# Token shift in two scaled terms: one on ScalarE into PSUM, one on VectorE

## The chip, the core and the metric

The kernel runs on one core of a Trainium2 chip. Its engines are TensorE (PE, matmul, with the weight load PEld shown apart), VectorE (DVE), ScalarE (ACT), GpSimd (POOL) and SyncE (SP, which issues the DMAs here). The metric is device time in microseconds of one execution; lower is better. Times of several runs are compared by their median.

## The reference, cut to what matters

One step of a decoder trunk with one layer, for a prompt of 1024 rows and 8 sample rows, all float32: a feed-forward block, a mixing block, a second feed-forward block. The mixing block projects each row to 3328 columns; the last 1792 of them, `pb`, feed a recurrent part, and this part begins with the token shift:

```python
def rwkv7_time_mix(pb, prev, s0, lp):
    shifted = jnp.concatenate([prev[:, None, :].astype(pb.dtype), pb[:, :-1]], axis=1)
    xs = pb + (shifted - pb) * lp['mu_shift']
    r, k, v, xw, xa, xg = jnp.split(xs, B_SPLITS, axis=-1)
    w = -jax.nn.softplus(-(lp['w0'] + jnp.tanh(xw) @ lp['w2']).astype(f32)) - 0.5
    a = jax.nn.sigmoid((lp['a0'] + xa @ lp['a2']).astype(f32))
    g = jax.nn.sigmoid(xg) @ lp['g2']
    ...
    s, y = wkv_scan(s0.astype(f32), r, decay, k, v, kk, a)
```

Each value is mixed with the value of the row before, with a weight `mu_shift` per column. The 1792 columns are 14 tiles of 128: four each of r, k and v, one that holds xw and xa, and one for xg.

## The kernel before, in words

Activations lie with features on the 128 partitions and tokens along the free axis. The prompt is cut into two halves of 512 rows (the first also carries the 8 samples). Each half goes through a first feed-forward phase (phases 0 and 1 of the trunk), the projection, the token shift and the recurrent part, the attention, the output projection, and a second feed-forward phase (trunk phases 2 and 3). Float32 products are made of three matmuls on split operands: weights come in as `raw`, ACT casts a high part, and POOL or DVE subtracts it for the low part (the tile `wts_w` for the feed-forward weights, `lin_w` for the projections).

Work is written as streams (generators): `trunk`, `wts`, `lin`, `proj`, `pre`, `tail`, `lora`, `job0` and `job1`, `attn`, `outn`, `dec` and so on. A planner (`Kern.run`, line 475) takes instructions from the streams and fixes the order on every engine before anything runs. It works with estimated costs (`price`, line 378) and, from the second pass on, with a latest time for each instruction, worked out backwards from the pass before (`latest`, line 564). `PASSES` (line 93) is the number of planning passes; the order of the last one is emitted. `BIAS` (line 94) adds microseconds to the latest times of a named stream, where the number is the how-manieth stream of that label it is (`tail1` is the second tail stream); a smaller latest time is taken first. Each engine runs its queue in the planned order. Because every instruction is emitted at one place, all have line 317 in the profile; tiles tell them apart, as `<stream>_<tile>`.

A PSUM tile is taken with `ps` or `ps2` (lines 238 and 245). Within a stream it comes from that stream's list of banks, in the order in which the program asks; a new tile in a bank waits for all uses of the tile before it. The jobs' first part has the bank `dec`, which the streams `pre`, `stats`, `decb` and others use too; later a job changes to `aux0` or `aux1`.

The token shift is `mixed` (line 1627). It is called twice in `s_lora` (line 1640) and three times in each `job` (line 1663, for k, r and v), four jobs to a half: 14 times a half, 28 in all. It loads a row tile from the scratch `PT` into E (one column more than 512, so that `E[:, 0:HS]` is the row before), POOL subtracts, and DVE scales and adds. The result goes to `out`, one of the tiles named `mix_T` in the profile, or `bset_la` and `bset_sg` for the two of `s_lora`. Within a job, the k tile comes first; the sums of squares for the key's norm go to a tile of the bank `dec`, and an inverse square root is worked out there in small DVE steps (line 1697); then the r tile is shifted (line 1698), the inverse norms are broadcast (line 1701) and turned by four transposes into another tile of that bank (line 1705); the v tile is shifted (line 1712) before the bonus term's matmul takes the bank (line 1716). The lock `front` lets one job, or `s_lora`, at a time use the shared input tiles.

Of the kernel before, what the change touches and what calls it, by code (L numbers as in the profile page):

```python
# [17 lines left out]
AF = mybir.ActivationFunctionType  # L18
ALU = mybir.AluOpType
# [3 lines left out]
P = 128  # L23
# [6 lines left out]
HS = 512  # L30
# [15 lines left out]
NB = 14  # L46
# [43 lines left out]
MW = 1  # L90
MARG = 0
SLACK = 0.02
PASSES = 2
BIAS = {"trunk2": 310, "outn3": -60, "outb0": 30, "pre2": -3, "outn0": -30, "rows0": -30, "job00": -10, "job03": 10, "stats0": 10, "dec0": 10, "wts3": 3, "pre3": -30, "mix1": -60, "lora1": 3, "attn11": 3, "tail2": 3}
SHIFT = {}
RESAT = 3
GROUPS = {(0, 10): [[0, 1, 2], [3, 4], [5, 6, 7], [8, 9]], (3, 6): [[0, 1, 2], [3], [4, 5]],
          (0, 8): [[0, 1, 2], [3, 4], [5], [6, 7]], (0, 6): [[0, 1, 2], [3], [4, 5]], (3, 4): [[0, 1], [2, 3]], (3, 8): [[0, 1, 2], [3, 4], [5], [6, 7]]}
# [29 lines left out]
def col(t):  # L128

    return t + TD * (t >= HS)  # L130
# [79 lines left out]
class Kern:  # L210
# [99 lines left out]
    def put(self, eng, op, fn, a, k):  # L310
# [14 lines left out]
        if o.late is not None:  # L325
            o.late += BIAS.get(st.part, 0) + sum(d for a, b, d in self.shift.get(st.part, ()) if a <= o.key[1] < b)
        self.price(o, op, a, k, outs[0], ins)
# [385 lines left out]
    def columns(self):  # L713

        nc, I = self.nc, self.I
        rows = self.E[:, :P]
        t = self.T(self.const, [P, P], "cols")
        r = 0
        for nm in ("n_ffn1_post", "n_mix_pre", "n_mix_post", "n_ffn2_pre", "n_ffn2_post",
                   "subln", "mu_shift", "w0", "a0", "k_k", "k_a", "r_k", "ln_x_w", "ln_x_b"):  # L720
            a = I[nm]
            if len(a.shape) == 3:
                a = a.rearrange("o h d -> o (h d)")
            k = a.shape[1] // P
            nc.sync.dma_start(rows[r:r + k, :], a[0].rearrange("(k p) -> k p", p=P))
            self.col[nm] = (t, r, k)
            r += k
        yield
        pt = self.ps2()
        nc.tensor.transpose(pt[:, :r], rows[:r], self.ident[:r, :r])  # L730
        nc.vector.tensor_copy(t[:, :r], pt[:, :r])
        for nm, k in (("n_ffn1_post", 0.5), ("n_ffn2_post", 0.5), ("subln", 1.0 - LAM_INIT), ("w0", 0.5), ("a0", 0.5)):
            nc.vector.tensor_scalar(self.vecs(nm), self.vecs(nm), k, None, ALU.mult)
        self.omka = self.T(self.const, [P, 4], "omka")
        nc.vector.tensor_scalar(self.omka, self.vecs("k_a"), -1.0, 1.0, ALU.mult, ALU.add)
        yield
# [57 lines left out]
    def stats(self, src, rb, tmp=("sqs", 1), **kw):  # L794

        for k in range(KT):
            self.square_sum(rb, src[k], k, self.tmp(*tmp, rb.shape[-1]), **kw)
        self.rstd(rb)

    def pair(self, k, src, gain, x):  # L800
# [573 lines left out]
    def s_loadx(self, half):  # L1374
# [28 lines left out]
        if half == 0:  # L1403
            yield ("wait", ("loaded", 0, "up", RESAT, None))
        for hf in range(2):
# [133 lines left out]
    def s_mix(self, half):  # L1539

        pool = self.pool
        yield ("wait", "setup")
        for m in (24, 25):
            yield ("wait", ("done", half, m))
        yield ("wait", ("staged", 1 + half))
        self.front = self.stage()
        self.spawn(self.s_lora(pool, half), "lora", 0)
        for i in range(4):
            self.spawn(self.s_job(pool, i, half), f"job{i % 2}", 0, "dec")
        self.sets = []  # L1550
        for j in range(2):
            if half:
                yield ("wait", "proj1")
            self.job_buffers(half, j)
            self.signal(("sets", half, j))
        for what in (f"jobs0_{half}", f"jobs1_{half}", f"rope{half}") + ("dec_b",) * half:
            yield ("wait", what)
        self.a_buffers(pool, half)
        self.spawn(self.s_prepare(pool, half), "prep", 0, "cb")
        for b in range(2):  # L1560
            self.spawn(self.s_attend(pool, half, b), f"attn{b}", 0, f"m{2 + b}", f"aux{b}")
        self.spawn(self.s_finish(pool, half), "fin", 0, "cb")
        if half:
            self.spawn(self.s_states(pool), "states", 2, "cb")
        self.spawn(self.s_out(half), "outb" if half else "out", 0, "m2", "m3")
# [61 lines left out]
    def mixed(self, pool, m, s, out, tag):  # L1627

        nc = self.nc
        t0 = col(s * HS)  # L1630
        E = self.first(tag, 1)
        nc.sync.dma_start(E[:, 1:], self.PT[12 + m][:, t0:t0 + HS])
        if s == 0:
            nc.gpsimd.memset(E[:, 0:1], 0.0)
        else:
            nc.sync.dma_start(E[:, 0:1], self.PT[12 + m][:, HS - 1:HS])
        nc.gpsimd.tensor_tensor(out, E[:, 0:HS], E[:, 1:], ALU.subtract)
        nc.vector.scalar_tensor_tensor(out, out, self.vec("mu_shift", m), E[:, 1:], ALU.mult, ALU.add)

# [297 lines left out]
    def s_decode_a(self):  # L1937
        yield ("wait", "setup")
        yield ("wait", ("staged", 1))
        yield ("wait", ("done", 0, 3))  # L1940
        yield ("wait", "lead")
        yield from self.a_decode()
        self.spawn(self.s_decode_b(), "decb", 1, "dec", ahead=8)

    def s_decode_b(self):
        yield ("wait", "proj0")
        take = self.arena(self.T(self.pool, [P, W_DEC], "dreg"))
        yield from self.b_decode(take, take, take(TD, C))
        self.signal("dec_b")

    def s_states(self, pool):

# [586 lines left out]
@with_exitstack  # L2539
def hymba_kernel(ctx, tc, I, O, late=None, dry=False):  # L2540
    K = Kern(ctx, tc, I, O, late, dry)
    K.setup()
    DR = lambda shape, tag: K.dram.tile(list(shape), F32, tag=tag, name=tag)
    K.res = DR([P, KT, NT], "res")
    K.PTall = DR([26, P, NT], "PT")
    K.PT = [K.PTall[m] for m in range(26)]
    K.YMall = DR([8, P, NT], "YM")
    K.YM = [K.YMall[m] for m in range(8)]
    K.Md = [DR([4, NC, 32, 32], f"Md{b}") for b in range(2)]
    K.Xd = [DR([4 * NC, 8, 4, 32], f"Xd{b}") for b in range(2)]  # L2550
    K.Dd = DR([160, P], "Dd")
    K.Qd = DR([32, P], "Qd")
    K.Ld, K.Lg = [DR([NF, P, D], f"Ld{i}") for i in range(2)], [DR([2, 12, P, D], f"Lg{i}") for i in range(2)]
    K.Li, K.Lo = DR([26, P, KT, P], "Li"), DR([KT, P, KT, P], "Lo")
    K.drams = {t.tensor.name: (tuple(t.shape), []) for t in (K.res, K.PTall, K.YMall, *K.Md, *K.Xd, K.Dd, K.Qd, O[3], *K.Ld, *K.Lg, K.Li, K.Lo)}
    K.c2 = K.const
    K.rows4 = K.T(K.const, [P, 1040], "rb")
    K.rb, K.prb = K.rows4[:, :520], K.rows4[:, 520:]
    K.E = K.T(K.const, [P, 520], "E")
    K.W, K.x, K.xt, K.ab = {}, {}, {}, {}  # L2560
    K.side = 0
    K.spawn(K.s_loadx(0), "ldx", 0, "cb", "dec")
    K.spawn(K.s_rownorm(0), "ssx", 0, RB)
    K.spawn(K.s_loadx(1), "ldxb", 3, "cb")
    K.spawn(K.s_rownorm(1), "ssxb", 3, RB)
    for ph in range(4):
        K.spawn(K.s_pre(ph), "pre", 0, "dec")
        if ph > 1:
            K.spawn(K.s_stats(ph), "stats", 1, "dec")
    K.asides = {}  # L2570
    for label in ("wts", "lin"):
        K.spawn(K.s_aside(), "keep", 0)
        K.asides[label] = K.streams[-1]
    K.spawn(K.s_weights(), "wts", 1)
    K.spawn(K.s_trunk(), "trunk", (0, 3), "m0", "m1")
    K.spawn(K.s_setup(), "setup", 2, "cb")
    for half in range(2):
        K.spawn(K.s_project(half), "proj", 0, "m2", "m3")
        K.spawn(K.s_rope(K.pool, half), "rope", 2)
        K.spawn(K.s_mix(half), "mix", 2)  # L2580
    K.spawn(K.s_decode_a(), "dec", 1, "cb", ahead=24)
    K.run()
    if dry:
        raise Planned(K.predicted, K.latest())
# [40 lines left out]
```

## Time and profile before

| | |
|---|---|
| median of 3 runs | 2302.5 us (2299.95 to 2308.67) |
| the profiled execution, its own time | 2294.3 us |
| its span, first to last instruction | 2292.3 us |
| mean granted TensorE clock | 0.991 |
| PE busy | 2228.0 us (97%) |
| DVE busy | 1556.5 us (68%) |
| ACT busy | 1078.0 us (47%) |
| POOL busy | 1021.6 us (45%) |

The profile is of one execution, so its times belong to the 2294.3 us of that execution. A line of a group gives the engine, the operation, output and inputs by tile names, shapes and count, then busy time, mean length of one, and the idle time of the engine just before them with what ended it. A line of a tile's instructions gives shortest, median and longest length in ns. A busy share of an engine is a mean over stages with different limits, so the stretches around an instruction say more than the page's first line.

### The profile page before, as it was taken

To read this page: it belongs to the slowest core of one execution; us is meant where nothing else is said; L and a number is where in the kernel's file an instruction comes from. 1 tells how busy PE (TensorE), PEld (TensorE's weight loads), DVE (VectorE), ACT (ScalarE), POOL (GpSimd) and SP (SyncE) were. 2 spreads that over 40 slices of the span, in tenths; PEclk is the share of its full clock that TensorE was granted. 3 is DMA by queue.
4 is the path that set the end of the run, shared out by engine and by line. 5 is a ranking of instruction groups with operands and counts; after the bars stand their busy time and mean duration, and the time that the engine had idled before them with its cause. 6 is when DMAs were issued, how large, how long until landed. Compare 5 with 4: busy or idle time off the path is not lost. (4 is left out here: it accounts for less than half of the span.)

```text
span 2292.3 us, 42829 instructions
## 1 busy us (share of the span) xinstructions
PE 2228.0 (97%) x15857; PEld 1985.3 (87%) x15857; DVE 1556.5 (68%) x3545; ACT 1078.0 (47%) x2231; POOL 1021.6 (45%) x846
## 2 busy tenths in 40 slices
PE   8999999999999999999899999999999999999998
PEld 7999999799887778988787867777788888999998
DVE  5477988756766687477866367665667356777776
ACT  5433443634354365434552145443665556544444
POOL 3344565534343566356543124333443254544443
PEclk9999999999999999999899999999999999999999
DMA  6423334344334576655679643324745847544543
GB/s 205 132 86 100 102 93 130 104 146 140 109 113 108 170 228 204 218 151 151 194 200 225 169 138 114 111 75 121 205 122 168 273 145 249 148 114 130 148 138 111
DMA packets 476295, 343.15 MB, mean 150 GB/s; under 512 B 82457, under 2 KB 424061, under 8 KB 476088
## 3 DMA queue, kind: packets, MB, share of 16 engines
q1 hardware_dynamic: 475480, 338.82, 50.8%
q8 instruction: 125, 2.05, 0.4%
q0 software_dynamic: 320, 1.08, 0.1%
q14 instruction: 82, 0.67, 0.1%
q10 hardware_dynamic: 288, 0.52, 0.1%
HBM read 278.98 MB, written 61.38 MB: 148 GB/s over the span
## 5 line engine op out<-in xcount | busy, mean ns | idle before, releaser
L317 PE MATMUL trunk_m<-trunk_xl,wts_w 128*128 128x256 f32 (+2 forms) x2700 | 459.4, 321 | 6.9 <-DVE trunk_xl L317 6.2
L317 POOL TENSOR_TENSOR wts_w<-wts_raw,wts_w 128x1024 fp32r<-128x1024 f32 (+2 forms) x162 | 314.4, 1948 | 318.1 <-ACT wts_w L317 279.4
L317 PE MATMUL trunk_m<-pre_X,wts_w 128*128 128x512 f32 (+3 forms) x2400 | 439.9, 335 | 5.7 <-POOL wts_w L317 2.8
L317 PEld LDWEIGHTS trunk_m<-trunk_xl,wts_w 128*128 128x128 f32 x2700 | 382.3, 189 | 42.3 <-DVE trunk_xl L317 7.9
L317 PEld LDWEIGHTS trunk_m<-pre_X,wts_w 128*128 128x128 f32 x2400 | 352.6, 190 | 48.2 <-issue 6.8
L317 PE MATMUL trunk_m<-pre_T,wts_w 128*128 128x512 f32 (+3 forms) x1848 | 362.8, 347 | 5.2 <-DVE trunk_xl L317 2.4
L317 ACT CAST wts_w<-wts_raw 128x1024 fp32r<-128x1024 f32 (+2 forms) x293 | 244.2, 848 | 237.9 <-PE trunk_m L317 162.1
L317 PEld LDWEIGHTS trunk_m<-pre_T,wts_w 128*128 128x128 f32 x1848 | 286.9, 190 | 43.7 <-issue 3.8
L317 DVE TENSOR_TENSOR trunk_xl<-trunk_xl,trunk_m 128x256 f32<-128x256 f32 (+2 forms) x351 | 165.8, 489 | 77.3 <-PE trunk_m L317 76.1
L317 PE MATMUL proj_m<-tail_xl,lin_w 128*128 128x256 f32 (+1 forms) x1248 | 168.5, 290 | 2.3 <-POOL lin_w L317 1.9
L317 PEld LDWEIGHTS proj_m<-tail_xl,lin_w 128*128 128x128 f32 x1248 | 155.6, 190 | 11.3 <-issue 7.0
L317 POOL TENSOR_TENSOR trunk_xl<-trunk_t,trunk_xl 128x512 fp32r<-128x512 f32 (+3 forms) x86 | 94.5, 1100 | 149.9 <-ACT trunk_xl L317 149.7
L317 PE MATMUL proj_m<-tail_T,lin_w 128*128 128x512 f32 (+1 forms) x672 | 153.1, 386 | 4.9 <-ACT tail_T L317 3.8
L317 PEld LDWEIGHTS proj_m<-tail_T,lin_w 128*128 128x128 f32 x672 | 122.6, 192 | 33.2 <-ACT tail_T L317 4.2
L317 DVE TENSOR_TENSOR wts_w<-wts_raw,wts_w 128x1024 fp32r<-128x1024 f32 (+2 forms) x101 | 108.1, 1071 | 35.1 <-ACT wts_w L317 34.4
L317 POOL TENSOR_TENSOR wts_w<-wts_lraw,wts_w 128x512 fp32r<-128x512 f32 x44 | 66.4, 1512 | 53.5 <-ACT wts_w L317 46.9
L317 ACT CAST wts_w<-wts_lraw 128x512 fp32r<-128x512 f32 x94 | 55.9, 617 | 64.7 <-DMA wts_lraw<-in_ffn_down_dram 33.4
L317 POOL TENSOR_TENSOR lin_w<-lin_raw,lin_w 128x1024 fp32r<-128x1024 f32 x19 | 45.9, 2417 | 79.4 <-ACT lin_w L317 69.7
L317 DVE TENSOR_TENSOR trunk_t<-trunk_g,trunk_m 128x512 f32<-128x512 f32 (+2 forms) x75 | 42.1, 562 | 53.4 <-PE trunk_m L317 50.7
L317 POOL TENSOR_TENSOR mix_T<-mix_T 128x512 f32<-128x512 f32 x32 | 38.6, 1207 | 79.2 <-DMA mix_T<-PT 54.6
L317 PE MATMUL trunk_aux<-trunk_xl,wts_w 128*128 128x256 f32 (+1 forms) x516 | 71.5, 283 | 0.0
L317 PE MATMUL trunk_m<-comb_T,wts_w 128*128 128x260 f32 x540 | 69.8, 283 | 0.0
(645 smaller groups left out, 4273.9 us busy)
## 6 DMA issues: line engine op xcount, KB each, us to landing
wts_raw<-in_ffn_gate_dram SPq DMA_DIRECT2D x88, 512.0 KB
wts_raw<-in_ffn_up_dram SPq DMA_DIRECT2D x58, 512.0 KB
wts_raw<-in_ffn_down_dram SPq DMA_DIRECT2D x56, 384.0 KB
wts_raw<-in_ffn_down_dram SPq DMA_DIRECT2D x29, 512.0 KB
lin_raw<-in_w_in_dram SPq DMA_DIRECT2D x26, 512.0 KB
wts_w<-Ld SPq DMA_DIRECT2D x22, 512.0 KB
mix_T<-PT SPq DMA_DIRECT2D x37, 256.0 KB
Ld<-wts_w SPq DMA_DIRECT2D x24, 384.0 KB
```

Source lines behind the costliest of these rows:

```text
L317: o = Op(eng, lambda: fn(*a, **k), st)
```

## The change: what it does

With w = `mu_shift`, the shifted tile is E0·w + E1·(1 - w), where E0 is the row before and E1 the row itself. A new vector `rest_mu` = 1 - w is made once at setup. `mixed` takes a PSUM tile; ACT writes E1·(1 - w) into it as a copy with a scale per partition, and DVE multiplies E0 by w and adds that tile. The subtraction on POOL is gone. `s_lora`, which had no PSUM bank, is given `dec`. The planner's settings differ too: four passes instead of two, and another, shorter list of offsets. Two further switches, `SWAP` and `SQP`, are 0, and their branches are not taken.

```diff
-PASSES = 2
-BIAS = {"trunk2": 310, "outn3": -60, "outb0": 30, "pre2": -3, "outn0": -30, "rows0": -30, "job00": -10, "job03": 10, "stats0": 10, "dec0": 10, "wts3": 3, "pre3": -30, "mix1": -60, "lora1": 3, "attn11": 3, "tail2": 3}
+PASSES = 4
+BIAS = {"trunk2": 300, "outn3": -60, "outb0": 30, "pre2": -3, "tail1": -30, "lora1": -10}
 SHIFT = {}
+SWAP = 0
+MIX = 1
+SQP = 0
...
+        self.rest_mu = self.T(self.const, [P, NB], "rmu")
+        nc.vector.tensor_scalar(self.rest_mu, self.vecs("mu_shift"), -1.0, 1.0, ALU.mult, ALU.add)
...
-        self.spawn(self.s_lora(pool, half), "lora", 0)
+        self.spawn(self.s_lora(pool, half), "lora", 0, "dec")
...
+        if MIX:
+            part = self.ps2()
+            nc.scalar.activation(part, E[:, 1:], AF.Copy, scale=self.rest_mu[:, m:m + 1])
+            nc.vector.scalar_tensor_tensor(out, E[:, 0:HS], self.vec("mu_shift", m), part, ALU.mult, ALU.add)
+            return
         nc.gpsimd.tensor_tensor(out, E[:, 0:HS], E[:, 1:], ALU.subtract)
         nc.vector.scalar_tensor_tensor(out, out, self.vec("mu_shift", m), E[:, 1:], ALU.mult, ALU.add)
```

More of the change, by code (lines that the diff above doesn't have):

```diff
@@ L796, in stats @@
         for k in range(KT):
-            self.square_sum(rb, src[k], k, self.tmp(*tmp, rb.shape[-1]), **kw)
+            if SQP:
+                self.square_sum(rb, src[k], k, self.ps2()[:, :rb.shape[-1]], engines=("vector",))
+            else:
+                self.square_sum(rb, src[k], k, self.tmp(*tmp, rb.shape[-1]), **kw)
         self.rstd(rb)
@@ L1941, in s_decode_a @@
         yield ("wait", "lead")
+        if SWAP:
+            yield ("wait", "decb")
         yield from self.a_decode()
-        self.spawn(self.s_decode_b(), "decb", 1, "dec", ahead=8)
+        if SWAP:
+            self.signal("dec_b")
+        else:
+            self.spawn(self.s_decode_b(), "decb", 1, "dec", ahead=8)
     def s_decode_b(self):
         yield ("wait", "proj0")
+        if SWAP:
+            yield ("wait", "setup")
+            yield ("wait", "lead")
         take = self.arena(self.T(self.pool, [P, W_DEC], "dreg"))
         yield from self.b_decode(take, take, take(TD, C))
-        self.signal("dec_b")
+        self.signal("decb" if SWAP else "dec_b")
     def s_states(self, pool):
@@ L2581, in hymba_kernel @@
     K.spawn(K.s_decode_a(), "dec", 1, "cb", ahead=24)
+    if SWAP:
+        K.spawn(K.s_decode_b(), "decb", 1, "dec", ahead=8)
     K.run()
```

## The prediction

> **What bounds the kernel now.** I read the page's busy times first, then TensorE's idle time in stretches, then its waits, and last the edited instructions themselves.
>
> ```profile
> span 2292.3 us, 42829 instructions
> PE 2228.0 (97%) x15857; PEld 1985.3 (87%) x15857; DVE 1556.5 (68%) x3545; ACT 1078.0 (47%) x2231; POOL 1021.6 (45%) x846
> L317 POOL TENSOR_TENSOR mix_T<-mix_T 128x512 f32<-128x512 f32 x32 | 38.6, 1207 | 79.2 <-DMA mix_T<-PT 54.6
> ```
>
> TensorE is busy for 2228.0 of 2292.3 us, so whatever is done to the other engines can at best remove 64.3 us of idle time, and the time in which TensorE runs at a reduced clock. The token shift adds no matmul, so it acts through this idle time alone. Stretches of 50 us (columns: length, then PE, PEld, DVE, ACT, POOL busy with counts, granted clock, DMA share, GB/s) say where the idle time lies:
>
> ```profile
> 350.00:400.00 50.00, 46.72 (x368) 45.67 (x367) 38.82 (x80) 21.35 (x44) 27.74 (x22) 0.97 0.43 129
> 400.00:450.00 50.00, 46.66 (x252) 39.63 (x252) 43.26 (x64) 34.63 (x62) 32.47 (x36) 1.00 0.36 107
> 450.00:500.00 50.00, 47.67 (x369) 45.98 (x368) 27.66 (x47) 14.44 (x18) 15.06 (x13) 0.97 0.48 144
> 1200.00:1250.00 50.00, 47.77 (x209) 37.15 (x208) 33.28 (x56) 12.18 (x14) 20.91 (x12) 1.00 0.99 242
> 1350.00:1400.00 50.00, 45.35 (x240) 34.19 (x238) 39.12 (x112) 27.64 (x50) 27.95 (x19) 1.00 0.56 159
> ...
> 1130.00:1135.00 5.00, 0.58 (x1) 0.29 (x1) 4.93 (x10) 2.54 (x5) 4.46 (x5) 0.82 0.98 303
> 1135.00:1140.00 5.00, 2.68 (x10) 2.49 (x10) 2.15 (x6) 2.16 (x6) 0.96 (x3) 0.50 0.90 309
> 1140.00:1145.00 5.00, 3.86 (x17) 3.71 (x18) 5.00 (x9) 3.23 (x8) 3.29 (x4) 0.50 0.58 169
> 1145.00:1150.00 5.00, 5.00 (x34) 4.79 (x33) 1.44 (x6) 2.64 (x7) 3.69 (x6) 0.82 0.87 255
> ```
>
> What touches the tile mix_T, which nearly all shifts use, in three long stretches (same columns):
>
> ```profile
> 440.00:700.00 260.00, 16.63 (x92) 10.90 (x92) 50.72 (x66) 39.13 (x68) 27.70 (x36) 0.99 0.43 125
> 1000.00:1200.00 200.00, 0.00 (x0) 0.00 (x0) 0.00 (x0) 0.00 (x0) 0.00 (x0) 0.97 0.61 177
> 1200.00:1520.00 320.00, 55.58 (x636) 45.63 (x637) 64.67 (x86) 62.83 (x143) 35.56 (x32) 1.00 0.55 148
> ```
>
> The reader should see two kinds of loss. Where the token shift works, a stretch of 50 us loses 2 to 5 us. The largest single hole, 1130 to 1145, is a change of phase, and no shift runs within 1000 to 1200. TensorE's waits name what it waits for there and elsewhere (us in total, times, longest):
>
> ```profile
> PE job_dec L317 <- DVE job_hres L317: 4.4, 2, 2.4
> PE proj_m L317 <- ACT tail_T L317: 3.8, 1, 3.8
> PE decb_dec L317 <- ACT decb_dreg L317: 3.0, 1, 3.0
> PE job_dec L317 <- DVE mix_T L317: 1.9, 1, 1.9
> ```
>
> Only the two waits of job_dec, 6.3 us together, are behind the code that the token shift feeds.
>
> **The change part by part.** The shift runs 28 times: 12 row tiles and two of the low-rank inputs, for each of two halves. Its instructions, by tile (ns min/median/max) and as groups (busy us, mean ns | idle before):
>
> ```profile
> L317 POOL TENSOR_TENSOR mix_T<-mix_T x32: 1035/1043/2037, 481.4 to 1502.9; 128x512 f32<-128x512 f32 x32
> L317 DVE SCALAR_TENSOR_TENSOR mix_T<-mix_T,setup_cols,mix_T x24: 732/746/2905, 483.8 to 1487.1; 128x512 f32<-128x512 f32 x24
> L317 DVE SCALAR_TENSOR_TENSOR bset_la<-bset_la,setup_cols,mix_T x2: 744/1820/2897, 469.2 to 1206.9; 128x512 f32<-128x512 f32 x2
> L317 DVE SCALAR_TENSOR_TENSOR bset_sg<-bset_sg,setup_cols,mix_T x2: 751/751/751, 479.1 to 1210.9; 128x512 f32<-128x512 f32 x2
> ...
> L317 DVE SCALAR_TENSOR_TENSOR mix_T<-mix_T,setup_cols,mix_T 128x512 f32<-128x512 f32 x24 | 22.2, 925 | 5.6 <-POOL mix_T L317 5.5
> L317 DVE SCALAR_TENSOR_TENSOR trunk_g<-trunk_t,trunk_m 128x512 f32<-128x512 f32 x40 | 27.3, 683 | 22.6 <-ACT trunk_t L317 22.5
> L317 DVE SCALAR_TENSOR_TENSOR trunk_g<-trunk_t,trunk_m 128x256 f32<-128x256 f32 x9 | 3.8, 417 | 8.9 <-ACT trunk_t L317 8.9
> L317 DVE SCALAR_TENSOR_TENSOR out_T<-out_T,setup_cols,outn_aux 128x256 f32<-128x256 f32 x16 | 6.9, 472 | 0.0
> L317 ACT ACTIVATE mix_T<-mix_T,setup_cols 128x512 f32<-128x512 f32 x8 | 5.8, 719 | 9.9 <-DVE mix_T L317 9.9
> L317 DVE TENSOR_TENSOR mix_T<-mix_T,job_dec x16: 676/684/690, 493.0 to 1490.3; 128x512 f32<-128x512 f32 x16
> ```
>
> *Removed.* POOL's 28 subtractions (24 of the group of 32, and two each into bset_la and bset_sg) at 1.043 us are 29.2 us. POOL is 45% busy, and this alone frees no TensorE time.
>
> *Added on ACT.* 28 scaled copies; the nearest row is the same operation with a scale per partition, 0.719 us, so 20.1 us, which takes ACT from 1078 to 1098 us (48%). Idle ACT time hides them; without that cover they cost the 20.1. No row shows such a copy with PSUM as its output, so I keep 0.719.
>
> *DVE.* One scalar_tensor_tensor stays, but its last operand moves to PSUM. The 683 of trunk_g has a PSUM operand and no scale per partition; the scale adds 472 - 417 = 55 ns at 256 columns. So 0.74 us, against the old median of 0.746: no gain by itself. But the old ones took 22.2 + 3.6 + 1.5 = 27.3 us in all, 6.4 us above 28 medians, because some took up to 2.9 us. Here is one (start, length):
>
> ```profile
> 469.19 2.39 POOL L317 TENSOR_TENSOR lin_w<-lin_raw,lin_w 128x1024 fp32r<-128x1024 f32 x1
> ...
> 469.23 2.90 DVE L317 SCALAR_TENSOR_TENSOR bset_la<-bset_la,setup_cols,mix_T 128x512 f32<-128x512 f32 x1 [1.11 <-POOL mix_T L317]
> ```
>
> DVE sat behind POOL's operation and ended 0.54 us after it. The group that reads PSUM (mix_T<-mix_T,job_dec) never exceeds 690 ns in 16 cases, so I count the 6.4 us as saved. DVE is 68% busy; this reaches TensorE only where DVE is late.
>
> *The chain.* A shift took 1.04 + 0.75 = 1.79 us and will take 0.72 + 0.74 = 1.46. Twelve of them stand at the head of a chain (two low-rank inputs and four keys in each half): 12 x 0.33 = 4.0 us earlier. Bounds: 0 if filler hides it, 4.0.
>
> *The bank.* The term needs a PSUM tile, which in a job is the bank "dec", in program order. The r tile's shift must now follow the inverse square root, whose scratch is in that bank, and the transposes must follow the shift. One such place today:
>
> ```profile
> 1357.33 0.75 DVE L317 SCALAR_TENSOR_TENSOR mix_T<-mix_T,setup_cols,mix_T 128x512 f32<-128x512 f32 x1
> 1357.56 2.18 POOL L317 TENSOR_TENSOR wts_w<-wts_raw,wts_w 128x768 fp32r<-128x768 f32 x1 [4.00 <-ACT wts_w L317]
> 1357.99 2.02 DVE L317 TENSOR_SCALAR mix_T<-job_stf 128x512 f32<-128x512 f32 x1
> 1360.16 0.63 PE L317 MATMUL job_dec<-init_ident,mix_T 128*128 128x128 f32 x4 [2.40 <-DVE job_hres L317]
> ...
> 1229.04 0.74 DVE L317 SCALAR_TENSOR_TENSOR mix_T<-mix_T,setup_cols,mix_T 128x512 f32<-128x512 f32 x1
> 1229.70 0.42 DVE L317 TENSOR_SCALAR mix_T<-job_stf 128x512 f32<-128x512 f32 x1
> 1230.26 0.63 PE L317 MATMUL job_dec<-init_ident,mix_T 128*128 128x128 f32 x4 [1.86 <-DVE mix_T L317]
> ```
>
> In the first, the r shift goes ahead, the broadcast behind it meets POOL, and TensorE waits 2.40 us. With the change ACT would work from about 1357.4 to 1358.15 and DVE to 1358.95, with the broadcast meanwhile: the transposes start some 1.1 us sooner. In the second they start at 1229.1 + 1.46 + hops = 1230.6, 0.35 us later. So 8 r shifts cost 8 x 0.35 = 2.8 us of chain; the upper bound is a place where the broadcast would have gone first, 1.46 less 0.42, or 1.04 x 8 = 8.3; the lower is -1.1 for the one place.
>
> The Trainium skill speaks against this part: "PSUM — Partial Sum Buffer", section "PSUM bank collisions raise a hardware error", says that two engines must not touch one bank and quadrant at once, even in disjoint columns, so the wait can't be planned away. By that rule alone the sum would carry the upper bound in place of the middle one, and come to about nothing. No run here shows a collision.
>
> *Waiting.* POOL waited 54.6 us for the shift's loads. Now the scaled copy waits on ACT, and behind it stand the casts that make weights ready for TensorE. No DMA is added, dropped or moved to another queue. The loads, and POOL's clearing of one column, stay; the extra vector 1 - mu is one small DVE instruction at setup, hidden.
>
> *The order.* All instructions are placed by a planner, so four planning passes instead of two, new offsets and other costs move everything. The one large new offset, 30 us earlier for tail1, is for the second chunk of the first phase's tail:
>
> ```profile
> L317 DVE SCALAR_TENSOR_TENSOR tail_xl<-tail_T,setup_cols,tail_xl x16: 395/962/2631, 422.1 to 445.8; 128x256 fp32r<-128x256 f32 x8, 128x264 fp32r<-128x264 f32 x8
> ```
>
> It stands in the stretches from 350 to 500, which lose 3.3 + 3.3 + 2.3 = 8.9 us. All of that could go, or as much be added; the bounds are -12 (the hole, below) and +10. I take a third of the 8.9, -3.0, a choice and not a finding.
>
> The sum: -1.1 at 1360, -4.0 for the heads, +2.8 for the bank, -3.0 for the order: -5.3 us. The profiled execution took 2294.3 us, 2.0 over its span, and would go to 2289. It lies 8.2 below the median of the three runs, 2302.5, and below their lowest; on the scale of the median the forecast is 2297.
>
> **The rivals.** *A better order fills the phase hole* (2285). From 1130 to 1145 TensorE idles 4.42 + 2.32 + 1.14 = 7.9 us, and the halved clock of the rows costs 2.68 x 0.5 + 3.86 x 0.5 + 5.0 x 0.18 = 4.2 more. If the new plan closes it, another 12.1 goes. For it: it is one place, and DVE is 4.93 of 5 busy there. Against: no shift runs there.
>
> *All is hidden* (2302). Shifts overlap trunk matmuls in nearly every place, and only 6.3 us of waits stand behind them.
>
> *The bank decides* (2310). 8.3 us of chain, less the 1.1 and without the heads' gain, is 7.2 over the median. Against: trunk matmuls fill in while job_dec waits.
>
> *ACT inherits POOL's waiting* (2317, slower). 54.6 / 32 x 28 = 48 us of waiting moves to ACT. ACT is busy 47% of the time, so about 22 us of casts get later; if half reaches TensorE, 11, plus the clock loss that the hole shows, 4: +15. It decides once loads land later than the planner thinks, by more than the two buffers for raw weights hold. Against: the planner sends to ACT what is ready first.
>
> **How the numbers follow.** Chances: forecast 0.32, better order 0.29, all hidden 0.17, ACT 0.14, bank 0.08. A measurement here tells no less than about 0.5%, or 11.5 us: 2291 to 2314 counts as the same. Faster takes the better order and a twentieth from the forecast, 0.34; slower takes ACT and another twentieth from the wide bounds of the order, 0.19; the rest is 0.47. The range leaves out a tenth at each side: 2278 (the better order and 7 us more) to 2316. The forecast's own range is 2290 to 2304.
>
> **What would show it.** Right: no shift on DVE above 0.8 us; ACT copies near 0.72; job_dec's wait on job_hres below 4.4; TensorE idle near 59 us. Wrong: shifts on ACT with DMA waits ahead of them and TensorE waiting for wts_w from ACT; transposes of job_dec waiting over 2 us on the shift; or a difference that lies at 1130 to 1150 or after 1800, where no shift runs: then the order, and not the shift, made it.

## The result, and the profile after

| | before | after |
|---|---|---|
| median of 5 runs | 2301.1 us (2294.3 to 2308.7) | 2285.6 us (2276.2 to 2287.0) |
| ratio, 95% interval | | 0.9923 [0.9903, 0.9942] |
| the profiled execution, its own time | 2294.3 us | 2287.0 us |
| mean granted TensorE clock | 0.991 | 0.995 |

The changed kernel is 0.8% faster, 15.5 us by the medians. The forecast was 2297.0, 5.5 below the median of 2302.5: the direction was right and the gain about three times as large as forecast. The measured median lies inside the whole range (2278 to 2316), but outside the forecast's own range (2290 to 2304) and below the 2291 under which the prediction would call it faster; 2285 was the price of its rival, the better order. The two profiled executions differ by only 7.3 us, since the one of before lies 7 us under its median; whatever is read from the two traces accounts for about half of the gain.

First the page of the changed kernel, its first lines (three lines of code were added above, so that line 317 is now 320):

```profile
span 2284.6 us, 42790 instructions
PE 2223.3 (97%) x15857; PEld 1981.1 (87%) x15857; DVE 1537.3 (67%) x3550; ACT 1098.8 (48%) x2256; POOL 986.9 (43%) x819
```

TensorE's idle time went from 64.3 to 61.3 us. Its busy time fell by 4.7 us with the same 15857 matmuls, because less of it ran at a reduced clock. Then the instructions of the shift, by tile and as groups (columns as in the prediction):

```profile
L320 ACT ACTIVATE job_dec<-mix_T,setup_rmu x24: 679/692/697, 483.1 to 1472.8; 128x512 f32<-128x512 f32 x24
L320 DVE SCALAR_TENSOR_TENSOR mix_T<-mix_T,setup_cols,job_dec x24: 733/747/750, 483.9 to 1473.6; 128x512 f32<-128x512 f32 x24
L320 ACT ACTIVATE lora_dec<-mix_T,setup_rmu x4: 672/692/692, 470.6 to 1195.3; 128x512 f32<-128x512 f32 x4
...
L320 DVE SCALAR_TENSOR_TENSOR mix_T<-mix_T,setup_cols,job_dec 128x512 f32<-128x512 f32 x24 | 17.9, 744 | 13.1 <-ACT job_dec L320 12.9
L320 ACT ACTIVATE job_dec<-mix_T,setup_rmu 128x512 f32<-128x512 f32 x24 | 16.6, 690 | 24.0 <-DMA mix_T<-PT 9.5 <-DVE job_stf L320 5.3 <-issue 3.5
```

The price of each instruction came out as forecast: 0.69 us on ACT (0.72 said), 0.744 on DVE (0.74 said), and no addition longer than 0.75 us, where before they took up to 2.9. ACT waited 9.5 us for the loads of 24 shifts and 3.3 for those of the other four (`lora_dec`), not the 48 of the rival in which it inherits POOL's waiting. TensorE's longest waits, and its stretches:

```profile
PE trunk_m L320 <- DVE trunk_xl L320: 6.3, 10, 2.2
PE job_aux L320 <- ACT mix_T L320: 2.3, 7, 0.6
```

```profile
350.00:400.00 50.00, 48.73 (x399) 47.90 (x398) 40.71 (x85) 21.20 (x43) 26.74 (x23) 1.00 0.42 128
400.00:450.00 50.00, 45.28 (x230) 38.19 (x230) 37.86 (x65) 31.94 (x61) 30.30 (x33) 0.93 0.33 101
450.00:500.00 50.00, 50.00 (x386) 47.79 (x385) 23.75 (x47) 17.45 (x23) 8.75 (x9) 1.00 0.49 142
1350.00:1400.00 50.00, 49.36 (x384) 38.20 (x383) 31.75 (x104) 30.14 (x56) 21.93 (x15) 1.00 0.50 142
...
1130.00:1135.00 5.00, 4.93 (x38) 4.49 (x36) 5.00 (x9) 2.54 (x4) 1.80 (x3) 1.00 0.91 283
1135.00:1140.00 5.00, 4.38 (x32) 3.93 (x32) 3.92 (x13) 2.88 (x8) 1.98 (x4) 1.00 0.92 273
1140.00:1145.00 5.00, 3.31 (x21) 2.67 (x20) 5.00 (x9) 3.55 (x9) 3.61 (x5) 1.00 1.00 341
1145.00:1150.00 5.00, 4.17 (x31) 3.72 (x30) 1.44 (x3) 3.63 (x7) 3.30 (x5) 1.00 0.43 137
```

The waits of job_dec, 4.4 and 1.9 before, are no longer in the list. 1350 to 1400, where shifts run, lost 4.65 us and now loses 0.64. The phase hole at 1130 is smaller too: 12.1 us of work in these 20 us, most of it at half clock, became 16.8 at full clock. Part of that came back next door, in the wider stretches:

```profile
1100.00:1200.00 100.00, 91.25 (x588) 82.62 (x587) 72.28 (x146) 53.49 (x101) 53.87 (x53) 0.93 0.67 190
```

```profile
1100.00:1200.00 100.00, 93.58 (x603) 84.05 (x603) 70.59 (x130) 60.03 (x106) 45.93 (x48) 0.98 0.64 194
```

(before, then after): 2.3 us less idle time and a clock of 0.98 in place of 0.93. So the traces show two gains, one where shifts run and one where none runs, and they cannot say which of the two parts of the change, the shift or the planner's settings, made either. That is what the runs had to separate.

### The profile page after: what moved, and what is told of

It is laid out like the page before. It is cut to its first block, busy times and chain, and to the rows that moved or that the text cites. A ratio compares the mean times of both kernels' runs of the same rounds, so it can differ in the third digit from the quotient of the medians.

```text
span 2284.6 us, 42790 instructions
## 1 busy us (share of the span) xinstructions
PE 2223.3 (97%) x15857; PEld 1981.1 (87%) x15857; DVE 1537.3 (67%) x3550; ACT 1098.8 (48%) x2256; POOL 986.9 (43%) x819
## 4 chain that ended last, share of the span: by engine, by line
PE 77%; DVE 6%; ACT 6%; DMA 5%; issue 3%; POOL 2%; SPq 1%; DVEq 0%; ACTq 0%; POOLq 0%
PE trunk_m L320 44%; PE proj_m L320 12%; PE trunk_aux L320 7%; PE job_aux L320 4%; PE out_m L320 2%; PE outb_m L320 2%; PE attn_m L320 2%; PE attn_aux L320 1%; SPq L320 1%; ACT wts_w L320 1%; ACT mix_T L320 1%; DMA wts_raw<-in_ffn_gate_dram 1%; PE job_dec L320 1%; DMA lin_w<-Lo 1%; POOL wts_w L320 1%
## 5 line engine op out<-in xcount | busy, mean ns | idle before, releaser
L320 POOL TENSOR_TENSOR lin_w<-lin_raw,lin_w 128x1024 fp32r<-128x1024 f32 x21 | 51.6, 2457 | 110.6 <-ACT lin_w L320 106.7
L320 POOL TENSOR_TENSOR wts_w<-wts_lraw,wts_w 128x512 fp32r<-128x512 f32 x43 | 60.0, 1398 | 45.2 <-ACT wts_w L320 41.9
L320 ACT CAST wts_w<-wts_dec 128x512 fp32r<-128x512 f32 x30 | 17.6, 587 | 103.7 <-DVE wts_dec L320 102.0
```

The costliest lines, as they stand in the source:

```text
L320: o = Op(eng, lambda: fn(*a, **k), st)
```

## The experiments

Two parts were changed at once: the *form* of the shift (which instructions) and the planner's *settings* (passes and offsets). The form changes the planner's order as well, since the planner prices it. So there are two kinds of run: one lets the planner make its own order, the other writes out the order that the planner had made for another kernel, with only the instructions of the shift exchanged in their places. In this second kind nothing else moves, except in one run, where a bank forces it (it is named there). The edits are cut to the lines that matter; the code that records an order and writes it out is left out. Ratios are against the kernel before on the same chip, whose medians were 2301.1, 2299.8 and 2302.5 us in the three groups of runs.

**One part at a time, the planner free.** The new form with the old settings, and the old form with the new ones (both as changes to the kernel after):

```diff
-PASSES = 4
-BIAS = {"trunk2": 300, "outn3": -60, "outb0": 30, "pre2": -3, "tail1": -30, "lora1": -10}
+PASSES = 2
+BIAS = {"trunk2": 310, "outn3": -60, "outb0": 30, "pre2": -3, "outn0": -30, "rows0": -30, "job00": -10, "job03": 10, "stats0": 10, "dec0": 10, "wts3": 3, "pre3": -30, "mix1": -60, "lora1": 3, "attn11": 3, "tail2": 3}
```

> The shift on ACT and DVE, planned with the settings of before (two passes, the long list of offsets). Theory S (the shift itself pays: no collisions with POOL, shorter chains): 2284 to 2292 us, a ratio of 0.991 to 0.996. Theory O (the order that the new settings make pays, above all in the hole at the change of phase near 1130 us): 2298 to 2305, ratio 0.998 to 1.002. Theory P (any new plan moves the time by some tenths of a per cent, whatever is changed): anywhere from 2290 to 2312.

```diff
-MIX = 1
+MIX = 0
```

> The old shift (POOL subtracts, DVE scales and adds), planned with the new settings (four passes, the short list). S: 2298 to 2305, ratio 0.998 to 1.002. O: 2284 to 2292, ratio 0.991 to 0.996. P: anywhere from 2290 to 2312.

Measured: 2322.5 us, ratio 1.0100 [1.0080, 1.0119], and 2309.3 us, ratio 1.0033 [1.0020, 1.0046]. Each part alone is slower than before; both together are faster. The first lies above everything that the three theories allowed, the second within P alone. By these four points the form of the shift is worth +21.4 us with the old settings and -23.7 us with the new ones. A saving of instructions can't have two signs, so what was measured here is mostly the order. In the first of the two runs TensorE's longest wait shows it:

```profile
PE trunk_m L320 <- DVE trunk_xl L320: 20.6, 14, 6.0
```

This is 14.3 us more than in the kernel after, between tiles of the feed-forward trunk that the shift does not touch.

**The changed kernel's order, the old form.** The planner plans with the new form, and the last step writes that order with the old one, POOL's subtraction standing where ACT's copy stood:

```diff
-    nc = build(plans[-1][2], False)
+    MIX = 0
+    Kern.order = At((k, i) for i, k in enumerate(done)), picks
+    nc = build(plans[-1][2], False)
```

> The exact order of the changed kernel on every engine, kept instruction by instruction, with the old shift put in: POOL's subtraction stands where ACT's scaled copy stood, and nothing else moves. S: the gain is lost for the most part, 2294 to 2301, and DVE shifts of up to 2.9 us are back. O: the gain stays, 2284 to 2290, whatever the shift is. P: as O.

Measured: 2297.2 us, ratio 0.9992 [0.9978, 1.0006]. The order with the old form is no faster than before, within the interval; exchanging the form inside it gains 11.6 us by the medians (by the two ratios, 0.69% or 16 us). The extra time arises where shifts run. The changed kernel and this run, in two long stretches that hold all shifts but the two low-rank ones near 1195:

```profile
440.00:700.00 260.00, 258.26 (x2298) 232.58 (x2298) 157.52 (x476) 126.39 (x234) 94.00 (x75) 1.00 0.43 124
1200.00:1520.00 320.00, 315.80 (x2007) 246.72 (x2007) 197.56 (x522) 138.09 (x249) 99.00 (x62) 1.00 0.55 147
```

```profile
440.00:700.00 260.00, 253.45 (x2214) 227.67 (x2212) 157.84 (x469) 113.13 (x213) 106.84 (x86) 1.00 0.42 122
1200.00:1520.00 320.00, 309.57 (x1816) 240.74 (x1815) 201.00 (x519) 122.22 (x217) 113.42 (x75) 0.99 0.55 147
```

TensorE works 4.81 and 6.23 us less in them, 11.0 together, against 10.4 us between the spans (2295.0 and 2284.6). Both runs have TensorE's instructions in the same order, so that each can be set beside its twin: this run falls 8.0 us behind from 500 to 750 and 10.6 from 1150 to 1500, and wins 5.7 back by 1950. The phase hole near 1130, on the other hand, is filled with the old form too, by 19.0 us of work in these 20 us (12.1 before, 16.8 in the changed kernel):

```profile
1130.00:1150.00 20.00, 19.01 (x129) 17.54 (x127) 17.65 (x34) 14.21 (x27) 8.54 (x13) 0.91 0.90 267
1350.00:1400.00 50.00, 47.81 (x273) 36.23 (x273) 31.67 (x111) 27.99 (x52) 27.83 (x19) 1.00 0.58 167
```

So that gain belongs to the order, and it alone did not make the kernel faster than before. 1350 to 1400 lies between the two: 2.19 us lost here, 4.65 before, 0.64 in the changed kernel. How a subtraction on POOL costs TensorE time can be followed at one place. First this run's DVE in order of time, then POOL:

```profile
1460.29 0.69 DVE L322 TENSOR_TENSOR job_w<-job_aux,bset_ct 128x512 f32<-128x512 f32 x1 [0.20 <-PE job_aux L322]
1462.40 0.75 DVE L322 SCALAR_TENSOR_TENSOR mix_T<-mix_T,setup_cols,mix_T 128x512 f32<-128x512 f32 x1 [1.43 <-POOL mix_T L322]
1463.07 0.68 DVE L322 TENSOR_TENSOR job_w<-job_cb,bset_ct 128x512 f32<-128x512 f32 x1
...
1474.86 0.19 DVE L322 TENSOR_TENSOR job_hres<-job_LT,job_aux 128x31 f32<-128x31 f32 x1 [2.46 <-DMA job_LT<-Md]
...
1475.87 0.68 DVE L322 TENSOR_TENSOR mix_T<-mix_T,job_aux 128x512 f32<-128x512 f32 x1
```

```profile
1459.00 2.37 POOL L322 TENSOR_TENSOR wts_w<-wts_raw,wts_w 128x1024 fp32r<-128x1024 f32 x1 [1.11 <-DMA mix_T<-PT]
1461.33 1.04 POOL L322 TENSOR_TENSOR mix_T<-mix_T 128x512 f32<-128x512 f32 x1
```

By 1459.0 the load is there, and POOL's queue has a weight subtraction of 2.37 us ahead of the shift's, which ends at 1462.37; DVE waits 1.43 us for it. Behind the addition, in DVE's queue, stands `job_w`, a product of the *other* job that has nothing to do with this shift; it goes through DRAM (`Md`) and comes back as `job_LT`. It is this load that DVE waits 2.46 us for, and TensorE in turn:

```profile
1476.60 1.30 PE L322 MATMUL job_aux<-job_w,mix_T 64*64 64x128 f32 x16 [2.08 <-DVE mix_T L322]
```

The same instructions in the changed kernel, DVE and then TensorE:

```profile
1449.94 0.69 DVE L320 TENSOR_TENSOR job_w<-job_aux,bset_ct 128x512 f32<-128x512 f32 x1 [0.20 <-PE job_aux L320]
1450.55 0.74 DVE L320 SCALAR_TENSOR_TENSOR mix_T<-mix_T,setup_cols,job_dec 128x512 f32<-128x512 f32 x1
1451.21 0.68 DVE L320 TENSOR_TENSOR job_w<-job_cb,bset_ct 128x512 f32<-128x512 f32 x1
...
1462.27 0.19 DVE L320 TENSOR_TENSOR job_hres<-job_LT,job_aux 128x31 f32<-128x31 f32 x1 [0.54 <-DMA job_LT<-Md]
...
1463.28 0.68 DVE L320 TENSOR_TENSOR mix_T<-mix_T,job_aux 128x512 f32<-128x512 f32 x1
```

```profile
1464.02 1.09 PE L320 MATMUL job_aux<-job_w,mix_T 64*64 64x128 f32 x16 [0.16 <-DVE mix_T L320]
```

From one `job_w` to the next DVE takes 1.27 us here and 2.78 there, and TensorE waits 0.16 us here and 2.08 there: from the first `job_w` to `job_hres` it is 12.33 and 14.57 us, so that of the 2.2 us between them 1.5 are the late `job_w` and 0.7 a slower trip through DRAM. A late shift holds DVE's queue, and what stands behind it reaches TensorE. This is one place, read from the trace; that it is the same at the others was not followed up.

**POOL's time or the late result?** The old subtraction can cost in two ways: POOL's own work comes later behind it, or its result comes late. The next run keeps the changed kernel and adds the 28 old subtractions on POOL, with nobody using what they give (`extra` keeps the numbering by which the order is written out):

```diff
             nc.scalar.activation(part, E[:, 1:], AF.Copy, scale=self.rest_mu[:, m:m + 1])
+            if not self.dry and not 8 <= m < 12:
+                self.extra = 1
+                nc.gpsimd.tensor_tensor(self.first("b"), E[:, 0:HS], E[:, 1:], ALU.subtract)
+                self.extra = 0
             nc.vector.scalar_tensor_tensor(out, E[:, 0:HS], self.vec("mu_shift", m), part, ALU.mult, ALU.add)
+            if not self.dry and 8 <= m < 12:
+                self.extra = 1
+                nc.gpsimd.tensor_tensor(E[:, 0:HS], E[:, 0:HS], E[:, 1:], ALU.subtract)
+                self.extra = 0
```

> The changed kernel in its own order, with the new shift, and beside it POOL still makes the 28 old subtractions, at the places they had in the run of the old shift in this order (the 8 for v stand behind the addition). Nothing uses their results, they only occupy POOL and its queue, waits for loads included. Theory P (the old shift cost 11.6 us in this order because POOL's other work, wts_w and lin_w, waits behind the subtraction): 2295 to 2299. Theory R (it cost that because the shifted tile itself comes late, POOL's own occupation being free): 2284 to 2288. A half-way value, 2290 to 2293, would say that both share it.

Measured: 2287.1 us, ratio 0.9937 [0.9917, 0.9957], against 0.9923 without them: Theory R. POOL waits for the loads as long as with the old form (47.6 us, against 46.1 in that run), and 16.0 us more for DVE; the two stretches are nearly whole:

```profile
L322 POOL TENSOR_TENSOR mix_T<-mix_T 128x512 f32<-128x512 f32 x36 | 43.1, 1198 | 67.4 <-DMA mix_T<-PT 47.6 <-DVE mix_T L322 16.0 <-DVE job_aux L322 3.7
```

```profile
440.00:700.00 260.00, 257.27 (x2287) 231.43 (x2287) 158.32 (x475) 125.76 (x233) 109.44 (x87) 1.00 0.43 124
1200.00:1520.00 320.00, 314.70 (x1933) 244.78 (x1933) 200.73 (x521) 137.37 (x247) 111.75 (x74) 1.00 0.55 146
```

TensorE loses 2.1 of the 11.0 us in them, and the span does not change (2284.8 against 2284.6). So 29 us of POOL's time, and waiting for loads in POOL's queue, cost next to nothing in this order. What is left for the 11.6 us is the late result, and the collisions of DVE with POOL, which the next run brings back.

**PSUM or SBUF.** Does it matter that the term lies in PSUM? In the changed kernel's order, ACT writes it to the result tile in SBUF and DVE adds in place, with two SBUF operands as before:

```diff
-            part = self.ps2()
+            part = self.ps2() if self.dry and MIX == 1 else out
```

> The exact order of the changed kernel; the new shift, but ACT writes its term into the SBUF tile of the result instead of PSUM, and DVE adds in place. Theory C (the 11.6 us that the old shift lost in this order came from collisions of DVE with POOL, which two SBUF operands allow): they come back, shifts of up to 2.9 us on DVE, 2292 to 2298. Theory L (they came from POOL's subtraction as such: later start and 0.35 us longer): the gain stays, 2283 to 2289.

Measured: 2285.6 us, ratio 0.9932 [0.9919, 0.9946], the same as with PSUM. The groups of DVE and ACT:

```profile
L322 DVE SCALAR_TENSOR_TENSOR mix_T<-mix_T,setup_cols,mix_T 128x512 f32<-128x512 f32 x24 | 25.7, 1070 | 11.0 <-ACT mix_T L322 10.9
L322 ACT ACTIVATE mix_T<-mix_T,setup_rmu 128x512 f32<-128x512 f32 x24 | 17.3, 721 | 11.8 <-DMA mix_T<-PT 9.1 <-POOL lin_w L322 2.5
```

The long additions are back, 1070 ns in the mean against 744, 7.8 us more of DVE in all, and the time does not move. This edit does two things, it brings the collisions back and takes the wait for the bank away; together they are worth nothing here, and neither was tested alone. Set beside its twin as above, TensorE falls 2.7 us behind from 500 to 700 and 1.7 from 1350 to 1400, and wins both back later, 4.4 us in all against the 18.6 of the old form. The late result is what is left, by exclusion and by the place followed above.

**The kernel before's order, the new form.** The mirror of the third run: planned with the old form, two passes and the old offsets, and written out with the new form, once with the term in PSUM (an instruction is moved back only where the bank's order forces it), once with the term in SBUF, which needs no bank:

```diff
+    MIX = 1
+    Kern.order = At((k, i) for i, k in enumerate(done)), picks
     nc = build(plans[-1][2], False)
```

> The order of the kernel before, kept instruction by instruction, with the new shift put in; only what the PSUM bank of the new term forbids is moved back to its first lawful place. S: 2288 to 2296. O: 2298 to 2306, and the hole at 1130 to 1145 is as before. The cost of the bank, if it is one, is here at its largest since nothing is planned around it: up to 8 us more.

```diff
-            part = self.ps2()
+            part = self.ps2() if self.dry and MIX == 1 else out
```

> The order of the kernel before, with the term on ACT written to SBUF, so that no bank is involved and nothing is moved. Theory B (the 43 us lost with the PSUM term in this order are the bank, one stall of 29 us near 1200 to 1300 above all): that stall is gone, 2294 to 2304. Theory W (ACT, waiting for the shift's loads, holds up what stands behind it): 2315 or more, with TensorE waiting on ACT's casts.

Measured: 2344.3 us, ratio 1.0182 [1.0162, 1.0202], with PSUM, far above all that was expected of it; 2302.0 us, ratio 1.0011 [0.9998, 1.0025], with SBUF, as Theory B said. The 42 us between the two (1.7% by the ratios, 39 us) are the bank's, and most of it is one wait of TensorE in the PSUM run. The wait, DVE ahead of it, and TensorE's stretches in it and behind it:

```profile
PE proj_m L322 <- DVE init_E L322: 29.3, 1, 29.3
```

```profile
1260.08 0.69 DVE L322 TENSOR_TENSOR decb_dreg<-decb_dreg 128x512 f32<-128x512 f32 x1 [7.60 <-DMA decb_dreg<-Dd]
...
1274.60 0.69 DVE L322 TENSOR_TENSOR decb_dreg<-decb_dreg 128x512 f32<-128x512 f32 x1 [6.17 <-DMA decb_dreg<-Dd]
...
1289.40 0.69 DVE L322 TENSOR_TENSOR decb_dreg<-decb_dreg 128x512 f32<-128x512 f32 x1 [6.89 <-DMA decb_dreg<-Dd]
...
1291.72 0.68 DVE L322 TENSOR_TENSOR init_E<-proj_m,init_rb 128x512 f32<-128x512 f32 x1
```

```profile
1265.00:1292.50 27.50, 0.00 (x0) 0.00 (x0) 11.15 (x17) 0.00 (x0) 3.00 (x2) 0.52 0.63 139
1292.50:1300.00 7.50, 6.97 (x16) 5.02 (x17) 6.84 (x10) 2.82 (x4) 0.57 (x1) 0.50 0.95 212
```

The stream `decb` shares the bank "dec" with the shift. In an order that was not made for it they line up: `decb` comes late, its products and their loads stand in one row in DVE's queue, and behind them `init_E`, for which TensorE waits 29.3 us. Then 7.0 us of TensorE work run at half clock, 3.5 us more. Without the bank the new form is worth nothing in this order (+0.1%). Its DVE waits point to why; the SBUF run's group beside the prediction's row, where the additions waited 5.6 us in all:

```profile
L322 DVE SCALAR_TENSOR_TENSOR mix_T<-mix_T,setup_cols,mix_T 128x512 f32<-128x512 f32 x24 | 21.9, 912 | 2.3 <-ACT mix_T L322 2.2
```

In the order of before, DVE hardly waited for POOL, 5.6 us over 24 shifts: the planner had put the additions where POOL was done. In the order made for ACT, the old form waits much more:

```profile
L322 DVE SCALAR_TENSOR_TENSOR mix_T<-mix_T,setup_cols,mix_T 128x512 f32<-128x512 f32 x24 | 22.7, 947 | 15.6 <-POOL mix_T L322 15.6
```

So the 11.6 us are not the price of the old form as such, but of the old form in an order that counts on the new one.

**How far do orders differ?** Five more runs with the planner free. Two drop `tail1` and `lora1` from the changed kernel's offsets and keep its four passes, one with each form:

```diff
-BIAS = {"trunk2": 300, "outn3": -60, "outb0": 30, "pre2": -3, "tail1": -30, "lora1": -10}
+BIAS = {"trunk2": 300, "outn3": -60, "outb0": 30, "pre2": -3}
```

> The new shift, planned with four passes and only the four offsets that both lists begin with (trunk2 300, outn3, outb0, pre2). To be read against the next kernel, which has the same settings. Theory S (the shift pays by itself in any plan): about 10 us below the next. Theory P (each plan is a draw, spread over some 20 to 30 us): anywhere from 2285 to 2320, and the pair's difference can have either sign.

> The old shift with the same settings as the kernel before this in the list. S: about 10 us above it. P: anywhere from 2285 to 2320.

(the second with `MIX = 0` beside it). Two change one setting of the changed kernel: `PASSES = 2` with its offsets, and four passes with the 16 offsets of before.

> New shift, the new short list of offsets, but two planning passes as before. With two passes and the old list the new shift took 2322.5 us, with four passes and the new list 2285.6. If the offsets made the difference: 2284 to 2292. If the passes made it: 2316 to 2326. If neither does it alone and an order is a draw among orders: anywhere from 2290 to 2315, and the next run no mirror of this one.

> New shift, the old long list of offsets, four planning passes. If the passes made the difference of 37 us between the two settings: 2284 to 2292. If the offsets made it: 2316 to 2326. If each order is a draw: anywhere from 2290 to 2315.

And one lets the planner make its own order for the SBUF form, with the changed kernel's settings:

```diff
-            part = self.ps2()
+            part = out
```

> The changed settings, but ACT writes the scaled term into the SBUF tile of the result and DVE adds in place, and the planner makes its own order for that, so that no shift uses the bank "dec". In the changed kernel's own order this form took 2285.6 us, the same as the PSUM form. If the freedom of the bank helps the planner: below 2283. If an order is a draw whatever the small edit: anywhere from 2285 to 2320, most likely near 2300, the middle of the eight orders seen so far.

The first pair has the sign of S, but half its size (5.9 us), and both are above before. The first half-way kernel (two passes) lies at the edge between two of its theories, the second in its draw; the SBUF form's own order is above everything that was expected of it.

All orders side by side, medians in us and ratios (the run with the 28 idle subtractions, 2287.1 us, is left out):

| form of the shift | order | median | ratio, interval |
|---|---|---|---|
| old | before's own | 2301.1 | 1 |
| old | two offsets dropped, 4 passes | 2317.0 | 1.0072 [1.0055, 1.0089] |
| old | new settings | 2309.3 | 1.0033 [1.0020, 1.0046] |
| old | written out from the changed kernel | 2297.2 | 0.9992 [0.9978, 1.0006] |
| new | new settings (the changed kernel) | 2285.6 | 0.9923 [0.9903, 0.9942] |
| new | two offsets dropped, 4 passes | 2311.2 | 1.0047 [1.0032, 1.0062] |
| new | 4 passes, old offsets | 2312.1 | 1.0045 [1.0028, 1.0063] |
| new | 2 passes, new offsets | 2315.1 | 1.0061 [1.0043, 1.0078] |
| new | old settings | 2322.5 | 1.0100 [1.0080, 1.0119] |
| new | written out from before | 2344.3 | 1.0182 [1.0162, 1.0202] |
| SBUF term | written out from before | 2302.0 | 1.0011 [0.9998, 1.0025] |
| SBUF term | written out from the changed kernel | 2285.6 | 0.9932 [0.9919, 0.9946] |
| SBUF term | its own, new settings | 2329.7 | 1.0123 [1.0102, 1.0145] |

Neither passes nor offsets alone make the gain: each of the two half-way kernels is 0.45 to 0.6% slower than before. The last two rows are the plainest: the same form of the shift and 44 us between two orders. Of the orders that the planner made for the new form one beats before, four don't. With the settings free the form is worth +21.4, -5.9 or -23.7 us, depending on the settings. No order that was run beats the changed kernel's. Why just this one is good is not settled; the runs show that it is, and by how much.

## Why the prediction was right, and where its sum was wrong

*Removed: POOL's 29.2 us free no TensorE time.* Right, and shown for the changed kernel's order: put back as idle work they cost 1.5 us by the medians, inside the intervals.

*Added on ACT: 20.1 us, hidden.* Right: 28 copies at 0.69 are 19.3 us, ACT went to 1098.8 us as said, and no TensorE wait of the list ends with one of them.

*DVE: 0.74 us, and 6.4 us of collisions saved.* Right in size: the collisions are gone. But they moved no time: with 7.8 us of them back, and the bank's wait gone, it stays at 2285.6.

*The chain: 12 heads, 4.0 us.* This step failed in size and in place. It took a shift as the sum of its two instructions, 1.79 and then 1.46 us. The trace shows it as two queues: the subtraction stands behind POOL's weight subtraction of 2.37 us, and other work stands behind the waiting addition on DVE. What this costs depends on the order: 11.6 us in the changed kernel's, nothing in the one of before (+0.1% for exchanging the form).

*The bank: +2.8, at most 8.3.* The middle was too high and the upper bound too low. Planned for, the bank costs nothing: the PSUM and SBUF forms agree to 0.1% in one order (with collisions in the one and the bank in the other), though ACT's copies do wait 5.3 us for the inverse square root (`job_stf`), as the step said. Not planned for, it costs 42 us, through `decb`, a stream that the step didn't look at. The Trainium skill's "PSUM — Partial Sum Buffer", section "PSUM bank collisions raise a hardware error", which was weighed there, says that two engines must not be in one bank and quadrant at once; that the wait can't be planned away was the prediction's own conclusion. The runs decide against that conclusion: the order of accesses stays, but its wait was hidden. No run here shows a collision.

*Waiting on ACT.* The rival fell: 9.5 us of waiting, and 2302.0 us in the order of before, where 2317 was its price.

*-1.1 us at 1360.* The wait of 2.40 us is gone from the list, but not by the step's reason: it is gone with the old form in the changed kernel's order too. With the PSUM form in the order of before the same matmuls wait 0.39 us, and there the broadcast still stands behind the shift; it took 0.42 us in place of 2.02, as POOL's weight subtraction began 0.1 us behind it, where before it began 0.4 ahead.

*The order: -3.0, within -12 to +10.* This is the term that was mis-sized. It was priced by the holes of one trace, as if the form's terms stood and an order came on top. The runs show orders of the new form from 2285.6 to 2322.5 and, of one form in SBUF, 44 us apart: the bounds should have been about -16 to +28 around the kernel before, and the forecast little more than which order comes out. The changed kernel's order with the old form lies 3.9 us under before, close to the -3.0, but that is no confirmation: its interval reaches no change. That -2.3 for the form and -3.0 for the order, added, gave the right sign is luck in good part: with the old settings the same form cost 21.4 us, and the new settings with the old form 8. What was gained is an exchange between the two that the sum has no term for.

*The stretches 350 to 500.* A third of 8.9 us was to go; idle time fell from 8.95 to 5.99, by 2.96, and the clock was about even (0.97, 1.00 and 0.97 became 1.00, 0.93 and 1.00). So the -3.0 was met at its place, though not in the sum. That `tail1` made it was not shown; the two kernels without `tail1` and `lora1` took 2311.2 and 2317.0.

*The rival "a better order fills the phase hole", 2285.* Its number was met, its reason in part: the hole shrank, and 1100 to 1200 gives back 2.3 us of idle time and 0.05 of clock. But the order alone, with the old form, fills the hole as well and is not faster than before. The gain needs order and form together.

*What would show it.* No addition above 0.8 us: yes. ACT near 0.72: 0.69. job_dec's wait below 4.4: yes, though the order alone does that. Idle time near 59: 61.3, with the rest in the clock, which this sign left out. "A difference at 1130 to 1150, then the order made it": the difference is there, and so is one where shifts run.

## What to carry to other kernels

When a planner or any list scheduler fixes the order, price a change of instructions as an exchange inside two orders, the old one and the new one, and give the order itself bounds from runs, since one trace's idle time bounds it too tightly (here 2286 to 2330 us for much the same work). An instruction on a slack engine can be costly not by its own time but by what stands ahead of it in that engine's queue and what stands behind its consumer in the next one: 28 subtractions were free as work and cost 11.6 us as a link, in the order that had no room for them. Before sharing a PSUM bank with one more stream, list all streams of that bank, and write an order for it.

## What the hardware showed beside that

The same scaled copy on ACT took 690 ns into PSUM (changed kernel) and 719 to 721 ns into SBUF (128x512, in three runs). The Trainium skill, "ScalarE: Activation LUTs", section "Step-by-step: what each stage is for", says that PSUM is the faster destination; the trace agrees, by 30 ns.

The addition on DVE took 733 to 750 ns in all 24 cases with one operand in PSUM, and 947 or 1070 ns in the mean with two SBUF operands in the changed kernel's order, the median there at 752. "SBUF — State Buffer", section "Who interferes with whom", in the Trainium skill states that a DVE instruction with two SBUF inputs contends with GpSimd's reads and that one with a single SBUF input, outside the modes that use two ports, does not. The trace agrees. In the changed kernel's order 7.8 us of such long additions, with the bank's wait taken away by the same edit, left the time as it was.

In and behind the one wait of 29.3 us the granted clock was 0.52 from 1265 to 1292.5 and still 0.50 from 1292.5 to 1300, over 6.97 us of TensorE work, so that the wait cost some 3.5 us beyond its own length.
